# Interleaving the small products of a blocked triangular inverse over tiles of the PE array

## The chip, the cores and the metric

One core of one Trainium2 chip runs the kernel. The metric is the device time of one execution, in microseconds. The kernel before the change was run three times: 1209.91, 1213.57 and 1215.92 us, median 1213.57 us.

## What is computed

The reference is one block of a transformer: modulated norm, two token mixers, a gated output product and a feed-forward network, for 512 tokens of `x` with 1024 channels and 256 tokens of context. The part that matters here is the second mixer, the gated delta rule, which runs over chunks of the tokens in both directions. Each chunk needs the inverse of a unit lower triangular matrix (the reference solves with it in chunks of 64):

```python
m = jnp.where(strict, jnp.einsum('nbhid,nbhjd->nbhij', kb, k) * gamma, 0.0)
t_inv = lax.linalg.triangular_solve(eye + m, jnp.broadcast_to(eye, m.shape), left_side=True, lower=True)
w_c = t_inv @ (kb * jnp.exp(gc)[..., None])
u_c = t_inv @ (v * beta[..., None])
def update(s, w_i, u_i, kd_i, ge_i):
    v_new = u_i - jnp.einsum('bhck,bhkv->bhcv', w_i, s)
    s_next = s * jnp.exp(ge_i)[..., None, None] + jnp.einsum('bhck,bhcv->bhkv', kd_i, v_new)
    return v_new, s_next
```

The scan over the chunks is run once for the context, whose final states start the scan over `x`.

## The kernel before, in words

The kernel works with chunks of 128 tokens and float32 products (dense products as three products of split operands). The delta rule is done in six groups of heads: `c0` and `c1` (four heads of the context each) and `x0` to `x3` (two heads of `x` each). A group has eight chunk matrices forward and eight backward. For each group the program runs, in this order of the text:

- `k_prep`: norms of the keys and the triangular matrices `YF` (forward) and `YB` (backward).
- `substitution`: the inverses of all 32x32 diagonal blocks, for two groups at once, as 30 steps on the vector engine (two instructions each, names `x0t`/`x0pr`, `x2t`/`x2pr`), with transfers to DRAM and back before and after (`c2` holds the inverses, `cT` their transposes).
- `levels` (line 1011): the inverses grow from 32 to 64 to 128. First 32-wide: `pz` (32 products, a 32x32 block of `Y` times `cT`), copied to `zt`, then `px` (48 products of `zt` and `c2`), copied into `YF` (forward inverse), `XB` (backward inverse) and `XV` (the transposes that the next level needs). The inverted diagonal blocks themselves are copied into `YF`, `XB` and `XV` too (twelve small copies, lines 1054 to 1057). Then 64-wide: `pz2` (eight products a direction), copied into the free halves of `YB` (line 1065), then `px2` (eight a direction), copied into `YF` (line 1077) and `XB` (line 1079). The trace gives a tile's name without its last number, so `pz2` is listed with `pz`, and `px2` with `px`; the shape 32x32 or 64x64 tells them apart.
- `scan`: chunk by chunk, the products `ks`, `qs`, `xr` (with the inverse), `ds` and `ow`, with small evictions between them (`R`, `vb`, `w`, `S`, `o`).

In this stretch the tensor engine keeps the order of the program's text. The steps of the delta rule wait on each other, so pieces of the dense stream (the k, q, v, z and gate products `b`, 128x512 each) are laid between them: `cover(place)` lays as many microseconds of it as the table `COVER` says for the place (`c1l` is the place between the steps of `levels` of group `c1`). Inside `levels`, `turn()` calls it. `pump(us)` moves a clock of the program's text on; what hangs on that clock (steps of a substitution, weight splits, transfers) is written into the text when its time has come, so a smaller `pump` puts such work later in the text. Copies through `so` and `vo` keep their place on the scalar and vector engine as well; each engine works its queue in order.

A product that reads 32 partitions and writes 32 partitions uses one 32x32 tile of the array: the tile's row is set by the partitions that its operands lie on, its column by the partitions of the result. Before the change `pz` runs all sixteen products of one tile (operands on partitions 0 to 31, result on 32 to 63) and then all sixteen of another (64 to 95, 96 to 127); `pz2` has both directions on one tile of 64x64 (operands on the lower 64 partitions, results on the upper).

Of the kernel before, what the change touches and what calls it, by code (L numbers as in the profile page):

```python
# [17 lines left out]
P = 128  # L18
# [8 lines left out]
# columns of the packed per-channel vectors  # L27
# [12 lines left out]
# constant matrices  # L40
# [3 lines left out]
# how much of the dense products is laid at each place between the steps of the delta rule  # L44
# [15 lines left out]
    "c0l": (0, 4.13, 0, 4.59, 1.61, 2.63,),  # L60
# [6 lines left out]
    "c1l": (0, 0.99, 0, 2.0, 1.23, 0.99,),  # L67
# [9 lines left out]
    "x0l": (0, 1.57, 0, 2.37, 1.38, 0,),  # L77
# [12 lines left out]
    "x1l": (0, 3.58, 0, 2.81, 1.95, 0,),  # L90
# [7 lines left out]
    "x2l": (0, 0.65, 0, 2.31, 1.31, 0,),  # L98
# [6 lines left out]
    "x3l": (0, 1.12, 0, 2.45, 1.0, 0,),  # L105
# [7 lines left out]
def block_kernel(ctx: ExitStack, tc: tile.TileContext, x, ctxin, vecs, consts, wmodA, wmodB, wk, wv, wq,  # L113
# [70 lines left out]
    class Wide:  # L184
        """two pages side by side"""
# [49 lines left out]
    AB = sm([P, 8, 4], "AB")  # A_x, A_c, B_x, B_c per channel tile: A = g (1 + scale), B = shift  # L235

    class ModPart:
        """channel tiles c0 .. c0 + nt - 1, both conditions: the shift, and with rows the scale too, as rows on the
        tensor engine; else the scale as partial sums on each partition; added up as columns"""
# [26 lines left out]
        def columns(self):  # L266
            """columns of pt: the shift (tile, condition), then the scale: (tile, condition) or (condition, tile)"""
# [9 lines left out]
        def part(self, c):  # L277
            """A and B of condition c"""
# [71 lines left out]
    # mixer A's v goes two k-tiles at a time while the rest of the modulation comes in  # L350
# [13 lines left out]
    def av_part(b, w, i, js=None):  # L364
        """two of the first four k-tiles; w holds these two alone"""
# [123 lines left out]
    # spatial weights, transposed: wst[j, g, i]  # L489
# [72 lines left out]
    def gates(act, nt, name):  # L562
        n = nt * 8
# [14 lines left out]
        # g = -exp(a_log) * softplus(ba + dt_bias)  # L578
# [77 lines left out]
    def tab(*a, **k):  # L656
        """functions that change the scalar engine's table keep their order"""
# [10 lines left out]
    class Group:  # L668
        """some heads of x or of the context; a page holds 512 / n heads (four chunks of 128 tokens)"""
# [924 lines left out]
def _ch(v):  # L1594
    """[.., n*128] -> [128, .. * n]"""
    return v.reshape(-1, P).T
# [58 lines left out]
```

## Time and profile before

| what | before |
|---|---|
| median of 3 runs | 1213.57 us (1209.91 to 1215.92) |
| span of the profiled execution | 1209.3 us |
| median less span | 4.3 us |
| TensorE (PE) busy | 1174.6 us, 97% of the span |
| VectorE (DVE) busy | 711.6 us, 59% |
| ScalarE (ACT) busy | 599.8 us, 50% |
| GpSimd (POOL) busy | 222.6 us, 18% |
| PE's share of the chain that ended last | 87% |

The profiled execution's own device time is not listed apart from its span; what lies around a span can only be told from the runs, whose fastest is 0.6 us and whose median is 4.3 us above it. Busy times overlap, so an engine's share tells little by itself; the chain that ended last follows the work back from the last instruction, and its lines in order of time say which engine each stretch waited for.

### The profile page before, as it was taken

Reading aid. Unit: us, or ns where it says so; the run is one execution under the profiler, and the core shown is the slowest. Engines: PE = TensorE matmul, PEld = TensorE weight load, DVE = VectorE, ACT = ScalarE, POOL = GpSimd, SP = SyncE. Lnnn points to the kernel's source line nnn. Section 1 sums busy time; section 2 is a strip of 40 time slices with the busy share of each in tenths; the row PEclk is TensorE's granted clock in tenths of the full one; section 3 lists DMA queues with packets and bytes.
Section 4 is the critical chain, followed back from the end, with each engine's and each line's share of the span. In section 5 each row is a group of like instructions: output and inputs, shape, how many; then the busy total and the mean of one; then the engine's idle time right before and its main releaser. Section 6 shows DMA issues by size and latency. Waiting matters only on the chain.

```text
span 1209.3 us, 20707 instructions
## 1 busy us (share of the span) xinstructions
PE 1174.6 (97%) x7964; PEld 1017.8 (84%) x7964; DVE 711.6 (59%) x1481; ACT 599.8 (50%) x1299; POOL 222.6 (18%) x380
## 2 busy tenths in 40 slices
PE   6999999999799999999999999999999999999997
PEld 2798788789688888888888887899888888889997
DVE  2845784537487586565796558776645454543442
ACT  4345253647774745568656473356534343331332
POOL 1330000106650454226521211000000000000020
PEclk9999899999899999999999999999999999999999
DMA  8784843232354322113234222575432222223321
GB/s 295 237 285 152 283 145 138 105 109 101 106 165 137 99 81 79 54 53 96 80 105 141 63 96 70 195 256 189 146 105 90 103 99 93 104 88 96 114 88 70
DMA packets 76904, 154.52 MB, mean 128 GB/s; under 512 B 30083, under 2 KB 36099, under 8 KB 76806
## 3 DMA queue, kind: packets, MB, share of 16 engines
q1 hardware_dynamic: 75078, 150.06, 37.5%
q10 hardware_dynamic: 1728, 3.15, 0.7%
q8 instruction: 62, 1.02, 0.3%
q14 instruction: 36, 0.29, 0.1%
HBM read 138.50 MB, written 14.68 MB: 127 GB/s over the span
## 4 chain that ended last, share of the span: by engine, by line
PE 87%; DVE 3%; ACT 3%; DMA 3%; issue 2%; POOL 2%; SPq 1%; ACTq 0%; DVEq 0%; POOLq 0%
PE v L814 5%; PE dn L1535 3%; PE dn L1534 3%; PE dn L1533 3%; PE b L814 3%; PE z L814 3%; PE k L814 3%; PE q L814 3%; PE fa L209 3%; PE fb L209 3%; PE fb L211 3%; PE fa L211 3%; PE fa L210 3%; PE fb L210 3%; PE wo L229 1%
## 5 line engine op out<-in xcount | busy, mean ns | idle before, releaser
L181 ACT CAST whi<-wr 128x512 fp32r<-128x512 f32 x216 | 133.3, 621 | 285.0 <-PE fa L210 62.1
L182 DVE TENSOR_TENSOR wlo<-wr,whi 128x512 fp32r<-128x512 f32 x200 | 137.2, 690 | 187.5 <-ACT whi L181 186.8
L1567 POOL TENSOR_TENSOR fj<-x2r,fg 128x768 f32<-128x768 f32 x4 | 7.7, 1954 | 437.2 <-DVE x2r L1562 437.2
L1534 PE MATMUL dn<-wlo,gh 128*128 128x256 f32 x288 | 81.5, 283 | 0.0
L1535 PE MATMUL dn<-whi,gl 128*128 128x256 f32 x288 | 81.5, 283 | 0.0
L1533 PE MATMUL dn<-whi,gh 128*128 128x256 f32 x288 | 81.5, 283 | 0.0
L209 PE MATMUL fa<-h2h,whi 128*128 128x512 f32 x160 | 62.3, 389 | 0.0
L210 PE MATMUL fa<-h2l,whi 128*128 128x512 f32 x160 | 62.3, 389 | 0.0
L211 PE MATMUL fa<-h2h,wlo 128*128 128x512 f32 x160 | 62.2, 389 | 0.0
L209 PE MATMUL fb<-h2h,whi 128*128 128x512 f32 x160 | 62.2, 389 | 0.0
L210 PE MATMUL fb<-h2l,whi 128*128 128x512 f32 x160 | 62.2, 389 | 0.0
L211 PE MATMUL fb<-h2h,wlo 128*128 128x512 f32 x160 | 62.2, 389 | 0.0
L1533 PEld LDWEIGHTS dn<-whi,gh 128*128 128x128 f32 x288 | 55.3, 192 | 0.0
L1534 PEld LDWEIGHTS dn<-wlo,gh 128*128 128x128 f32 x288 | 55.3, 192 | 0.0
L1535 PEld LDWEIGHTS dn<-whi,gl 128*128 128x128 f32 x288 | 55.3, 192 | 0.0
L662 ACT ACT_TABLE_LOAD x39 | 50.0, 1283 | 7.4 <-DVE cvk L753 3.0
L429 DVE SCALAR_TENSOR_TENSOR mac<-wmb,cond,mac 128x1024 f32<-128x1024 f32 x30 | 39.3, 1312 | 4.5 <-DMA wmb<-wmodB 4.1
L229 PE MATMUL av<-whi,hxh 128*128 128x256 f32 x128 | 36.8, 288 | 0.7 <-ACT hxh L325 0.7
L231 PE MATMUL av<-whi,hxl 128*128 128x256 f32 x128 | 36.3, 285 | 1.1 <-DVE hxl L326 1.1
L230 PE MATMUL av<-wlo,hxh 128*128 128x256 f32 x128 | 36.2, 283 | 0.0
L211 PEld LDWEIGHTS fa<-h2h,wlo 128*128 128x128 f32 x160 | 30.1, 188 | 6.3
L211 PEld LDWEIGHTS fb<-h2h,wlo 128*128 128x128 f32 x160 | 30.0, 188 | 6.3
(1517 smaller groups left out, 3646.3 us busy)
## 6 DMA issues: line engine op xcount, KB each, us to landing
wr<-wup SPq DMA_DIRECT2D x42, 512.0 KB, 3.3
wmb<-wmodB SPq DMA_DIRECT2D x32, 512.0 KB, 6.7
wr<-wout SPq DMA_DIRECT2D x16, 512.0 KB, 3.9
wr<-wdn SPq DMA_DIRECT2D x16, 512.0 KB, 3.5
wm<-wmodA SPq DMA_DIRECT2D x16, 256.0 KB, 5.8
x<-x SPq DMA_DIRECT2D x8, 512.0 KB, 6.5
wm<-wmodA SPq DMA_DIRECT2D x8, 512.0 KB, 6.0
wr<-wu SPq DMA_DIRECT2D x8, 512.0 KB, 3.4
```

The costliest lines, as they stand in the source:

```text
L181: nc.scalar.copy(dst_hi, src)
L182: eng.tensor_tensor(dst_lo, src, dst_hi.bitcast(F32), op=ALU.subtract)
L209: mm(ps, lhsT=lh, rhs=rh, start=start, stop=False)
L210: mm(ps, lhsT=lh, rhs=rl, start=False, stop=False)
L211: mm(ps, lhsT=ll, rhs=rh, start=False, stop=stop)
L229: mm(ps, lhsT=a, rhs=wh[:, s], start=first and k == 0, stop=False)
L429: nc.vector.scalar_tensor_tensor(a, raw, cond[:, k, 0:1], a, op0=ALU.mult, op1=ALU.add)
L662: ins = nc.scalar.activation(*a, **k)
L814: tc.keep_in_program_order(mm(*a, **k))
L1533: mm(pss4[t][:, :256], lhsT=a, rhs=wh[:, s], start=k == 0, stop=False)
L1534: mm(pss4[t][:, :256], lhsT=a, rhs=wl[:, s], start=False, stop=False)
L1535: mm(pss4[t][:, :256], lhsT=c, rhs=wh[:, s], start=False, stop=k == NF - 1)
```

## The change

The same products are computed, and as many copies are made. In `levels` four things change.

- The loops are turned inside out. `pz` alternates between its two tiles, `px` between three, and `pz2` and `px2` between the two directions.
- The backward product of `pz2` is written to the lower 64 partitions; its copy into `YB` moves it to the upper 64.
- Copies start when all products of a stage are laid, no longer when half of them are. The second of the two `zt` copies goes from the scalar to the vector engine. The twelve copies of the diagonal blocks come behind `pz`; before they came behind `px`.
- `turn()` is called four times instead of six, and the table loses the two zeros, so the dense stream gets the same times at the same four places (after `pz`, `px`, `pz2`, `px2`). `pump` gets 0.6 four times, where it got 0.4 or 0.6 eight times.

Comments and docstrings are dropped elsewhere. The diff, cut to its core:

```diff
-    "c1l": (0, 0.99, 0, 2.0, 1.23, 0.99,),
+    "c1l": (0.99, 2.0, 1.23, 0.99),
...
-    "x0l": (0, 1.57, 0, 2.37, 1.38, 0,),
+    "x0l": (1.57, 2.37, 1.38, 0),
...
         pz = [chb(f"{name}pz{j}") for j in range(2)]
-        for j in range(2):
-            a, b = 2 * j, 2 * j + 1
-            sa, sb = slice(32 * a, 32 * a + 32), slice(32 * b, 32 * b + 32)
-            for m in range(16):
-                Y3 = YF3 if m < 8 else YB3
+        for m in range(16):
+            Y3 = YF3 if m < 8 else YB3
+            for j in range(2):
+                sa, sb = blk32[2 * j], blk32[2 * j + 1]
                 pmm(pz[j][sb, m * 32:m * 32 + 32], lhsT=Y3[sa, m % 8, sb], rhs=cT[sa, m], start=True, stop=True)
-            pump(0.4)
-            sc.copy(zt[sb].rearrange("p m c -> p (m c)"), pz[j][sb])
-            turn()
+        pump(0.6)
+        for j, copy in enumerate((sc.copy, ve.tensor_copy)):
+            sb = blk32[2 * j + 1]
+            copy(zt[sb].rearrange("p m c -> p (m c)"), pz[j][sb])
+        for bb in range(4):
+            bs = blk32[bb]
+            so.copy(YF3[bs, :, bs], c2[bs, Fm])
+            so.copy(XB3[bs, :, bs], cT[bs, Bm])
+            lb = slice(32 * (bb % 2), 32 * (bb % 2) + 32)
+            vo.tensor_copy(XV3[bs, :, lb], cT[bs, Fm] if bb < 2 else c2[bs, Bm])
+        turn()
         px = [scb(f"{name}px{j}") for j in range(2)]
-        for j in range(2):
-            a, b = 2 * j, 2 * j + 1
-            sa, sb = slice(32 * a, 32 * a + 32), slice(32 * b, 32 * b + 32)
-            for m in range(16):
-                ms = slice(m * 32, m * 32 + 32)
-                fwd = m < 8
+        for m in range(16):
+            ms = slice(m * 32, m * 32 + 32)
+            fwd = m < 8
+            for j in range(2):
+                sa, sb = blk32[2 * j], blk32[2 * j + 1]
                 if fwd or j == 1:
                     pmm(px[j][sa, ms], lhsT=zt[sb, m], rhs=c2[sb, m], start=True, stop=True)
                 if (not fwd) or j == 0:
                     pmm(px[j][sb, ms], lhsT=c2[sb, m], rhs=zt[sb, m], start=True, stop=True)
-            pump(0.6)
+        pump(0.6)
+        for j in range(2):
...
-            for bb in (a, b):
-                bs = slice(32 * bb, 32 * bb + 32)
-                so.copy(YF3[bs, :, bs], c2[bs, Fm])
-                so.copy(XB3[bs, :, bs], cT[bs, Bm])
-                lb = slice(32 * (bb % 2), 32 * (bb % 2) + 32)
-                vo.tensor_copy(XV3[bs, :, lb], cT[bs, Fm] if bb < 2 else c2[bs, Bm])
-            turn()
+        turn()
...
-        for d in range(2):
-            pz2 = scb(f"{name}pz2{d}")
-            for s in range(8):
-                pmm(pz2[hi64, s * 64:s * 64 + 64], lhsT=(YF3, YB3)[d][lo64, s, hi64], rhs=XV3[lo64, s] if d == 0 else XB3[lo64, s, lo64], start=True, stop=True)
-            pump(0.4)
-            (sc.copy if d == 0 else ve.tensor_copy)(z2[d][hi64], p3(pz2, 8)[hi64])
+        pz2 = [scb(f"{name}pz2{d}") for d in range(2)]
+        for s in range(8):
+            ss = slice(s * 64, s * 64 + 64)
+            pmm(pz2[0][hi64, ss], lhsT=YF3[lo64, s, hi64], rhs=XV3[lo64, s], start=True, stop=True)
+            pmm(pz2[1][lo64, ss], lhsT=YB3[lo64, s, hi64], rhs=XB3[lo64, s, lo64], start=True, stop=True)
+        pump(0.6)
+        sc.copy(z2[0][hi64], p3(pz2[0], 8)[hi64])
+        ve.tensor_copy(z2[1][hi64], p3(pz2[1], 8)[lo64])
         turn()
...
+        px2 = [scb(f"{name}px2{d}") for d in range(2)]
+        for s in range(8):
+            ss = slice(s * 64, s * 64 + 64)
+            pmm(px2[0][lo64, ss], lhsT=z2[0][hi64, s], rhs=YF3[hi64, s, hi64], start=True, stop=True)
+            pmm(px2[1][hi64, ss], lhsT=XV3[hi64, s], rhs=z2[1][hi64, s], start=True, stop=True)
+        pump(0.6)
```

How the rows of two engines move, in group `c1` and in group `x0`. On the tensor engine the products of `pz2` of group `c1` stand so before (`c1pz` is their result, `c1XV`, `c1XB`, `c1YF`, `c1YB` the operands; `z` is the dense stream, behind it `px2`):

```order
L814 MATMUL c1pz_4674<-c1XV,c1YF 64x64 x8
L814 MATMUL c1pz_4687<-c1XB,c1YB 64x64 x8
```

and so in the change, the first eight of sixteen:

```order
L814 MATMUL c1pz_4671<-c1XV,c1YF 64x64
L814 MATMUL c1pz_4672<-c1XB,c1YB 64x64
L814 MATMUL c1pz_4671<-c1XV,c1YF 64x64
L814 MATMUL c1pz_4672<-c1XB,c1YB 64x64
L814 MATMUL c1pz_4671<-c1XV,c1YF 64x64
L814 MATMUL c1pz_4672<-c1XB,c1YB 64x64
L814 MATMUL c1pz_4671<-c1XV,c1YF 64x64
L814 MATMUL c1pz_4672<-c1XB,c1YB 64x64
```

Forward and backward alternate now; `pz`, `px` and `px2` change in the same way, and the dense pieces between the four stages keep their number and place in every group. In `x3`, whose stages also have products `pb` of the next phase between them, 23 of these stand ahead of the scan before the change, and 25 in it.

On the vector engine, behind the last product of the scan of `c0` (`c02s1ds`, whose results update the states `c02s0S`), the queue at `levels(c1)` is before:

```order
L1170 SCALAR_TENSOR_TENSOR c02s0S_4435<-c02s0S_4435,cexs,c02s1ds 128x128
L1170 SCALAR_TENSOR_TENSOR c02s0S_4437<-c02s0S_4437,cexs,c02s1ds 128x128
L649 TENSOR_TENSOR x0t_4576<-x0pr 128x228
L1045 COPY c1YF<-c1px_4583 32x8x32
L991 TENSOR_TENSOR x0pr<-x0pr,x0t_4576 128x12x19
L1045 COPY c1YF<-c1px_4584 32x8x32
L649 TENSOR_TENSOR x0t_4609<-x0pr 128x220
L1048 COPY c1XV<-c1px_4583 32x8x32
L991 TENSOR_TENSOR x0pr<-x0pr,x0t_4609 128x11x20
L649 COPY c1XV<-c1cT 32x8x32 x2
```

and in the change:

```order
L1172 SCALAR_TENSOR_TENSOR c02s0S_4432<-c02s0S_4432,cexs,c02s1ds 128x128
L1172 SCALAR_TENSOR_TENSOR c02s0S_4434<-c02s0S_4434,cexs,c02s1ds 128x128
L1033 COPY c1zt<-c1pz_4535 32x512
L649 COPY c1XV<-c1cT 32x8x32 x2
L649 COPY c1XV<-c1c_4233 32x8x32 x2
L649 TENSOR_TENSOR x0t_4586<-x0pr 128x234
L991 TENSOR_TENSOR x0pr<-x0pr,x0t_4586 128x13x18
L1055 COPY c1YF<-c1px_4592 32x8x32
L649 TENSOR_TENSOR x0t_4642<-x0pr 128x228
L1055 COPY c1YF<-c1px_4593 32x8x32
L991 TENSOR_TENSOR x0pr<-x0pr,x0t_4642 128x12x19
L1058 COPY c1XV<-c1px_4592 32x8x32
```

A copy of `zt`, for which `px` waits, now stands behind the state updates, and the substitution of `x0` is one step later in the queue.

On the scalar engine, behind the last eviction of `v_prep(x0)` (`x0v`), the queue at `levels(x0)` is before:

```order
L662 ACT_TABLE_LOAD
L662 ACTIVATE b_5054<-b_4895 128x512
L649 CAST wq1hi<-wq1r 128x512
L1030 COPY x0zt<-x0pz_5075 32x512
L1030 COPY x0zt<-x0pz_5076 32x512
L1046 COPY x0XB<-x0px_5126 32x8x32
L649 COPY x0YF<-x0c_4907 32x8x32
L649 COPY x0XB<-x0cT 32x8x32
```

and in the change:

```order
L662 ACT_TABLE_LOAD
L662 ACTIVATE b_5054<-b_4895 128x512
L649 CAST wq1hi<-wq1r 128x512
L1033 COPY x0zt<-x0pz_5075 32x512
L649 COPY x0YF<-x0c_4935 32x8x32
L649 COPY x0XB<-x0cT 32x8x32
L649 COPY x0YF<-x0c_4935 32x8x32
L649 COPY x0XB<-x0cT 32x8x32
```

One `zt` copy is gone from this queue, the other still stands behind the table load, and the eight diagonal copies (four shown) come ahead of the copies out of `px`.

## Rows read from the trace of the kernel before

**Rows 1.** From the page: the tensor engine's busy time, share of the span and instructions, and the shares of the chain that ended last by engine.

```profile
PE 1174.6 (97%) x7964; PEld 1017.8 (84%) x7964; DVE 711.6 (59%) x1481; ACT 599.8 (50%) x1299; POOL 222.6 (18%) x380
...
PE 87%; DVE 3%; ACT 3%; DMA 3%; issue 2%; POOL 2%; SPq 1%; ACTq 0%; DVEq 0%; POOLq 0%
```

**Rows 2.** Busy time by stretch, for `levels` of `c1` and `x0`, and the sum over the six stretches of `levels`. Columns: stretch, its length, then busy us and instructions of PE, PEld (weight loads), DVE, ACT and POOL, PE's granted clock, DMA share, GB/s.

```profile
443.70:457.10 13.40, 13.40 (x247) 11.44 (x246) 10.27 (x26) 6.75 (x16) 4.47 (x7) 1.00 0.18 61
482.90:497.80 14.90, 14.90 (x253) 12.70 (x253) 7.23 (x14) 11.17 (x25) 4.16 (x10) 1.00 0.27 73
...
sum 96.10, PE 96.00 PEld 81.04 DVE 53.15 ACT 66.47 POOL 31.97; mean PE 16.00 PEld 13.51 DVE 8.86 ACT 11.08 POOL 5.33
```

**Rows 3.** The chain that ended last, in order of time, over `levels(c1)`. Columns: start us, us, what, and how many records (a float32 product is two records).

```profile
443.71 2.04 PE c1pz L814 x64
445.75 1.36 PE z L814 x5
447.11 2.04 PE c1px L814 x96
449.15 2.49 PE z L814 x10
451.64 2.02 PE c1pz L814 x32
453.66 1.58 PE z L814 x6
455.25 1.82 PE c1px L814 x32
```

**Rows 4.** Single records of the tensor engine in `px` (first two) and at the change of direction in `px2` (last two) of `c1`, in order of time. Columns: start us, us, engine, line, operation, result and operands, tile, shape.

```profile
447.12 0.19 PE L814 MATMUL c1px<-c1c,c1zt 32*32 32x32 f32 x1
447.13 0.19 PE L814 MATMUL c1px<-c1zt,c1c 32*32 32x32 f32 x1
...
455.93 0.27 PE L814 MATMUL c1px<-c1YB,c1XV 64*64 64x64 f32 x1
455.98 0.22 PE L814 MATMUL c1px<-c1YF,c1YB 64*64 64x64 f32 x1
```

**Rows 5.** The tensor engine alone by stretch: most of the first half of `pz` of `c1` (one tile), and the first 32 records of `px` of `c1` (eight forward matrices, two tiles in turn). Columns: stretch, length, busy us and records, granted clock, DMA share, GB/s.

```profile
443.64:444.62 0.98, 0.98 (x34) 1.00 0.39 134
447.04:447.54 0.50, 0.50 (x32) 1.00 0.90 369
```

**Rows 6.** Vector and scalar engine at `levels(c1)`, in order of time. Columns as in rows 4; in brackets the idle time before and what ended it.

```profile
444.88 0.59 DVE L649 TENSOR_TENSOR x0t<-x0pr 128x234 f32<-128x234 f32 x1
...
446.14 0.59 DVE L1170 SCALAR_TENSOR_TENSOR c02s0S<-c02s0S,cexs,c02s1ds 128x128 f32<-128x128 f32 x2
...
449.21 0.42 DVE L1045 COPY c1YF<-c1px 32x256 f32<-32x256 f32 x1 [0.21 <-PE c1px L814]
...
450.96 0.57 DVE L649 COPY c1XV<-c1cT 32x256 f32<-32x256 f32 x2
...
453.70 0.69 DVE L1065 COPY c1YB<-c1pz 64x512 f32<-64x512 f32 x1 [0.68 <-PE c1pz L814]
```

**Rows 7.** Scalar engine at `levels(x0)`, in order of time.

```profile
481.60 2.18 ACT L962 ACTIVATE x0v<-x0vt,xrk 128x128 f32<-128x128 f32 x8
483.80 1.28 ACT L662 ACT_TABLE_LOAD   x1
485.10 0.60 ACT L662 ACTIVATE b<-b 128x512 f32<-128x512 f32 x1
485.59 0.61 ACT L649 CAST wq1hi<-wq1r 128x512 fp32r<-128x512 f32 x1
486.23 1.18 ACT L1030 COPY x0zt<-x0pz 32x512 f32<-32x512 f32 x2
...
489.13 0.41 ACT L649 COPY x0YF<-x0c 32x256 f32<-32x256 f32 x1
...
489.85 0.41 ACT L649 COPY x0YF<-x0c 32x256 f32<-32x256 f32 x1
```

**Rows 8.** The chain that ended last over the end of `levels(x0)`: `px2`, and the first product with the inverse.

```profile
495.90 1.83 PE x0px L814 x32
...
499.94 0.11 PE x00s0xr L814
```

**Rows 9.** Vector engine at the end of `levels(x0)`, in order of time.

```profile
495.79 0.75 DVE L752 SCALAR_TENSOR_TENSOR cvq<-q,vec,cvq 128x511 f32<-128x511 f32 x1 [0.25 <-ACT cvq L749]
...
497.95 0.70 DVE L1079 COPY x0XB<-x0px 64x512 f32<-64x512 f32 x1
498.85 0.35 DVE L1134 SCALAR_TENSOR_TENSOR x00s0R<-x00s0ks,xexs,x0v 128x128 f32<-128x128 f32 x1 [0.20 <-PE x00s0ks L814]
```

**Rows 10.** Scalar engine at `levels(x3)`: the copy out of `pz2` and the squares behind it.

```profile
718.56 0.58 ACT L1065 COPY x3YB<-x3pz 64x512 f32<-64x512 f32 x1
719.17 1.15 ACT L1189 ACTIVATE osq<-o 128x512 f32<-128x512 f32 x2
```

**Rows 11.** The tensor engine's edge between the dense stream and `px` in `c1`: two dense products and the first small one.

```profile
446.48 0.40 PE L814 MATMUL z<-hxh,wz7lo 128*128 128x512 f32 x1
446.71 0.40 PE L814 MATMUL z<-hxh,wz7hi 128*128 128x512 f32 x1
447.04 0.21 PE L814 MATMUL c1px<-c1c,c1zt 32*32 32x32 f32 x1
```

More of the change, by code (lines that the diff above doesn't have):

```diff
@@ L59 @@
     "x1p": (0,),
-    "c0l": (0, 4.13, 0, 4.59, 1.61, 2.63,),
+    "c0l": (4.13, 4.59, 1.61, 2.63),
     "c00s2": (0.83, 0.8,),
@@ L89 @@
     "x3p": (0,),
-    "x1l": (0, 3.58, 0, 2.81, 1.95, 0,),
+    "x1l": (3.58, 2.81, 1.95, 0),
     "x12s1": (1.06, 0.67, 1.69, 1.72,),
@@ L97 @@
     "og": (0.29, 4.73, 0.08, 9.7, 1.3, 1.3, 1.3, 1.3,),
-    "x2l": (0, 0.65, 0, 2.31, 1.31, 0,),
+    "x2l": (0.65, 2.31, 1.31, 0),
     "x24s1": (0.18, 0.51, 0.42, 0.2,),
@@ L104 @@
     "x3v": (1.66, 0,),
-    "x3l": (0, 1.12, 0, 2.45, 1.0, 0,),
+    "x3l": (1.12, 2.45, 1.0, 0),
     "x36s1": (0, 0, 0, 0.13,),
@@ L1021, in levels @@
         zt = pg("gr", f"{name}zt").rearrange("p (m c) -> p m c", m=16)
+        blk32 = [slice(32 * i, 32 * i + 32) for i in range(4)]
         pz = [chb(f"{name}pz{j}") for j in range(2)]
-        for j in range(2):
-            a, b = 2 * j, 2 * j + 1
-            sa, sb = slice(32 * a, 32 * a + 32), slice(32 * b, 32 * b + 32)
-            for m in range(16):
-                Y3 = YF3 if m < 8 else YB3
-                pmm(pz[j][sb, m * 32:m * 32 + 32], lhsT=Y3[sa, m % 8, sb], rhs=cT[sa, m], start=True, stop=True)
-            pump(0.4)
-            sc.copy(zt[sb].rearrange("p m c -> p (m c)"), pz[j][sb])
-            turn()
-        px = [scb(f"{name}px{j}") for j in range(2)]
-        for j in range(2):
-            a, b = 2 * j, 2 * j + 1
-            sa, sb = slice(32 * a, 32 * a + 32), slice(32 * b, 32 * b + 32)
-            for m in range(16):
-                ms = slice(m * 32, m * 32 + 32)
-                fwd = m < 8
+        for m in range(16):
+            Y3 = YF3 if m < 8 else YB3
+            for j in range(2):
+                sa, sb = blk32[2 * j], blk32[2 * j + 1]
+                pmm(pz[j][sb, m * 32:m * 32 + 32], lhsT=Y3[sa, m % 8, sb], rhs=cT[sa, m], start=True, stop=True)
+        pump(0.6)
[9 more added lines that the diff above has]
+        turn()
+        px = [scb(f"{name}px{j}") for j in range(2)]
+        for m in range(16):
[3 more added lines that the diff above has]
+                sa, sb = blk32[2 * j], blk32[2 * j + 1]
                 if fwd or j == 1:
@@ L1066, in levels @@
-        turn()
-        for d in range(2):
-            px2 = scb(f"{name}px2{d}")
-            for s in range(8):
-                ss = slice(s * 64, s * 64 + 64)
-                if d == 0:
-                    pmm(px2[lo64, ss], lhsT=z2[d][hi64, s], rhs=YF3[hi64, s, hi64], start=True, stop=True)
-                else:
-                    pmm(px2[hi64, ss], lhsT=XV3[hi64, s], rhs=z2[d][hi64, s], start=True, stop=True)
-            pump(0.4)
-            if d == 0:
-                sc.copy(YF3[lo64, :, hi64], p3(px2, 8)[lo64])
-            else:
-                ve.tensor_copy(XB3[hi64, :, lo64], p3(px2, 8)[hi64])
+        pz2 = [scb(f"{name}pz2{d}") for d in range(2)]
@@ L1080, in levels @@
+        pump(0.6)
+        sc.copy(YF3[lo64, :, hi64], p3(px2[0], 8)[lo64])
+        ve.tensor_copy(XB3[hi64, :, lo64], p3(px2[1], 8)[hi64])
         turn()
@@ L1089, in block_kernel @@
     class Chain:
+        pass
     def feed(g, heads, step):
```

1 line of the change is left out of this document (added).

## The prediction

> **What bounds the kernel now.** I read the page first, then the busy time by stretch, the chain of waits, and single records. The page gives the tensor engine 97% of the span and 87% of the chain [rows 1]. In the six stretches of `levels` together it is busy 96.00 of 96.10 us, the vector engine 53.15 and the scalar engine 66.47 [rows 2]; nothing waits visibly. So in these stretches the tensor engine is the bound, and a shorter stream of products shortens the kernel, as long as the copies between the four stages stay hidden under the dense pieces.
>
> The stages themselves: in `c1` `pz` holds the engine 2.04 us, `px` 2.04, `pz2` 2.02 and `px2` 1.82, with 5, 10 and 6 dense products between them [rows 3]: 7.92 us a group, 47.5 us in six groups. These 224 records are short of work: in `pz`, all on one tile, 34 records take 0.98 us, some 30 ns each, while in the part of `px` that already takes two tiles in turn 32 take 0.50 us, 15.6 ns each [rows 5]. Single records show how: two on different tiles start 0.01 us apart, each 0.19 us long [rows 4].
>
> **The change, part by part.** *Products.* `pz`: 64 records on two tiles at 30 ns a tile and record are 32 x 0.031 = 1.0 us; with the edge 1.04, so 1.0 saved. `pz2`: 32 records on one tile are 2.0 us; on two tiles 1.02, so 1.0 saved. `px2`: its directions already lie on two tiles, and where one takes over from the other they overlap: the backward direction starts at 455.93, before a forward record at 455.98 [rows 4]. Alternating all the way gives some 0.95, so 0.87 saved. `px` mixes: today half of it alternates. With three tiles in turn its fullest tile has 32 records, so the floor is 1.0 us; if records never come closer than 15.6 ns its 96 take 1.5 us. I take 1.25, as starts 0.01 us apart leave room for a third tile: 0.79 saved. Sum 3.7 us a group, between 3.4 and 3.95.
>
> Here a rule speaks against the change. The 64-wide pairs read the same partitions and differ in the columns of the array, and so do the pairs in `px` that run at 15.6 ns [rows 5]. The Trainium skill ("TensorE: Matmul & The Clock Gate", part 3, The mechanism) says that a weight load overlaps with products in flight only when the row group differs. By that rule `pz2` and `px2` would stay at 2.0 and 1.8 us; the trace disagrees for the 32-wide pairs, and the overlap at 455.93 disagrees for the 64-wide.
>
> *Copies.* None is added. What changes is the start: copies wait for the whole stage, and the stage is shorter, so against the end of a stage nothing is lost. One `zt` copy moves from the scalar engine (0.59 us a copy [rows 7]) to the vector engine; nearest prices there are 0.42 us for half its columns and 0.69 for as many [rows 6]; I take 0.65. The copy that moves 64 partitions to the other half has no row; 0.69 is its floor, twice that its ceiling, and I take 0.69, since only the start partition differs. The ceiling would cost up to 0.7 us where it is waited for, 4.2 in all. The twelve diagonal copies leave the way from `px` to `pz2`, good, but the eight on the scalar engine (0.72 us a pair [rows 7]) now stand ahead of whatever comes next there.
>
> *Where the cover no longer reaches*, replayed in the clock of the old trace:
>
> `c0`, `x1`: their dense pieces are long (over 3 us after `pz` and `px`); the replay finds nothing exposed. 3.6 each.
>
> `c1`: `pz` would end at 444.75 and five dense products let `px` start at 446.1. But the new `zt` copy stands on the vector engine behind the state updates, the last of which end at 446.7 [rows 6]; so `zt` is there at 447.3, and `px` starts no sooner than now (447.11). That eats the whole saving of `pz`. Then `px` ends near 448.6, four `XV` copies (0.57 us for two [rows 6]), four substitution instructions and three evictions of some 0.4 us each bring `XV` to about 451.1; `pz2` starts at 451.2, 0.4 before today. Its backward copy, behind three more substitution instructions and a weight split, is done near 454.1; `px2` runs from 454.2 to 455.15 and today ends at 457.07. Saved: 1.9 of 3.7. Queued behind the waiting copy on that engine is the substitution of `x0`, one step later than before; its result is needed only at `x0pz`, some 30 us later.
>
> `x0`: `zt` on the scalar engine is behind the evictions of `v`, a table load, a sigmoid and a cast, which end at 486.23 and none of which wait for `pz` [rows 7]; so `px` starts at 486.9, where it is 487.07 now. `px` to 488.15, twelve dense products (2.96), `pz2` to 492.1, seven (1.81), `px2` to 494.9 instead of 497.73 [rows 8]. Then the vector engine binds: two taps, a split and the `XB` copy run back to back from 495.79 to 498.65 [rows 9]; the taps follow the dense block's end, about 1.7 us behind `pz2`, so the row moves to 493.8 and ends at 496.7, four `R` at 0.26 follow, and the first product with the inverse starts at 497.9 instead of 499.94. Saved: 2.0.
>
> `x2`: the diagonal copies (2.9 us) delay a weight cast and the split behind it, and with it `XV`, 0.3 us past the cover. Saved: 3.4.
>
> `x3`: the copy out of `pz2` waits behind eight diagonal copies (2.9), a table load (1.3), a sigmoid (0.6), two `XB` (0.7), squares (0.6 [rows 10]) and two casts (1.2), so it runs when it does today, at 718.6 [rows 10]; what of `pb` is pulled ahead counts as saved. 3.0.
>
> Sum: 3.6 + 1.9 + 2.0 + 3.6 + 3.4 + 3.0 = 17.5 us. The smaller `pump` only moves substitution steps one place later; everything else shifts along. The profiled span of 1209.3 would become 1191.8; the median of the runs stands 4.3 above that span, and 1213.57 - 17.5 = **1196.0 us**.
>
> **Rivals.** (A) The forecast.
>
> (B) Everything stays hidden: my replays are too strict, for instance because the vector engine starts a copy earlier than I put it. 6 x 3.7 = 22 us, 1191.4. For it: no wait shows today [rows 2]. Against: the two queues in the order of the change.
>
> (C) The copies bind in most groups, as in `c1` and `x0` or worse (the shifted 64-partition copy at its ceiling, more queueing on the scalar engine): 1.0 to 1.9 us a group, 6 to 11 us, about 1205. For it: the scalar engine is busy 11.17 of 14.90 us in `x0` [rows 2], and after the change of 11.2.
>
> (D) Only pairs on different partitions overlap (the rule above). As a mechanism here: `pz` saves 1.0, the third tile in `px` 0.5, the 64-wide stages nothing, and in `c1` and `x0` `pz`'s part is lost: about 6 us, 1207. Against: rows 4 and 5.
>
> (E) The change does not do what it says: the engine takes its queue strictly in order and the alternation is not used. Then the products cost what they cost, and the lost head start of the first half's copies adds about 1 us: 1214.6. Against: rows 4.
>
> (F) Slower. Each change of tile costs what the edge between dense and small products costs: 0.33 us from start to start instead of 0.23 [rows 11], 0.1 us. `pz` would have some 32 changes, `px` 48, `pz2` and `px2` 16 each: 112 x 0.1 = 11.2 us a group against 7.9, 20 us more in all, 1233. It decides once the mean spacing over the 224 records passes 35 ns. Against: `px` changes its tile at nearly every record at 15.6 ns.
>
> **How the numbers follow.** A 0.58, B 0.12, C 0.18, D 0.04, E 0.04, F 0.04. A, B and most of C (0.15) lie more than 0.5% (6.1 us) below today, which is about what a measurement of this kernel can tell from no change: faster 0.85. The rest of C with D and E: same 0.11. Slower 0.04. The range reaches from all hidden with `px` at its floor (6 x 3.95 = 23.7 us, 1190) to the weaker part of C, 7.5 us saved: 1190 to 1206.
>
> **What would show it.** In the changed profile `pz` should take about 1.0 us for 64 records, `px` 1.0 to 1.5 for 96, `pz2` 1.0 and `px2` 0.95 for 32. `px` of `c1` should wait for the vector engine's `zt`, `px` of `x0` for the scalar engine's, `xr` of `x0` for `R`. The stretch from the first `pz` to the scan should shrink by 3.5 us in `c0` and `x1` and by about 2 in `c1` and `x0`, and what lies between the groups should keep its length. The prediction is wrong if the 64-wide stages keep 2 us (D), if records alternate at 30 ns (E), or if waits of some us appear ahead of `px` or `px2` in all groups (C).

## The result, and the profile after

The changed kernel takes 1194.57 us (median of 4 runs, 1192.69 to 1199.92) against 1211.97 before: a ratio of 0.9875, 95% interval 0.9848 to 0.9902. A second comparison, of 6 runs with 11, gave 0.9896 (0.9875 to 0.9917). The prediction was 1196.0, within 1190 to 1206. The change makes the kernel faster: by 15.1 us in the first comparison and 12.6 in the second. The forecast of 17.5 was too high, by 3.6 us against the 13.9 that the traces show below, and its median came nearer than its sum deserved.

The page's two lines that answer to [rows 1]:

```profile
PE 1152.9 (97%) x7964; PEld 995.5 (84%) x7964; DVE 714.5 (60%) x1487; ACT 595.8 (50%) x1293; POOL 223.2 (19%) x380
...
PE 83%; DVE 5%; ACT 4%; DMA 4%; issue 2%; POOL 2%; SPq 1%; ACTq 0%; POOLq 0%; DVEq 0%
```

The tensor engine is busy 21.7 us less (some 4 of them belong to the first trace of the kernel before alone, in which the clock fell once more; its second trace has 1170.8); its share of the chain falls from 87 to 83%, and the vector engine's rises from 3 to 5%. The products became cheap enough for copies to be waited for. The stages, in the chain of the changed kernel over `levels(x1)`, where the tensor engine waits for nothing (columns as in rows 3):

```profile
565.26 1.13 PE x1pz L814 x64
...
570.47 1.14 PE x1px L814 x95
...
575.00 1.08 PE x1pz L814 x32
...
578.58 1.08 PE x1px L814 x32
```

4.43 us, where [rows 3] add up to 7.92. The single records of the first two products of `pz2` show why (start us, us):

```profile
574.93 0.27 PE L814 MATMUL x1pz<-x1XV,x1YF 64*64 64x64 f32 x1
574.94 0.27 PE L814 MATMUL x1pz<-x1XB,x1YB 64*64 64x64 f32 x1
575.04 0.22 PE L814 MATMUL x1pz<-x1XV,x1YF 64*64 64x64 f32 x1
575.05 0.22 PE L814 MATMUL x1pz<-x1XB,x1YB 64*64 64x64 f32 x1
```

Forward and backward start 0.01 us apart. But the tensor engine now waits in the stretches, where it waited for nothing [rows 2]. Its waits there, and one in the scan of `x1` (us in total, times, longest):

```profile
PE c1pz L814 <- DVE c1XV L1058: 1.1, 1, 1.1
...
PE x0pz L814 <- ACT x0v L962: 0.8, 1, 0.8
PE c1px L814 <- DVE c1zt L1033: 0.7, 1, 0.7
...
PE x12s1ks L814 <- DVE c02s0S L1172: 0.6, 1, 0.6
...
PE x2pz L814 <- DVE x2XV L1058: 0.4, 1, 0.4
PE x3pz L814 <- DVE x3XV L1058: 0.3, 1, 0.3
```

**A ruler that is finer than the runs.** Runs scatter by several us; the starts of single products do not, once counted from the first product of `pz` in `c0`. The table gives us from the first product of a group's `pz` to its first product with the inverse (`xr`), from the first `xr` of `x1` to `pz` of `x2`, and the stretch from the first `pz` of `c0` to the first product of the feed-forward. Everything that the change touches lies in that stretch. The other columns belong to the experiments below.

| | before | after | loops_only | one_half | grain | wide | mixed_now |
|---|---|---|---|---|---|---|---|
| c0 | 23.0 | 19.5 | 20.2 | 20.5 | 20.8 | 19.3 | 19.6 |
| c1 | 14.7 | 13.5 | 11.6 | 14.1 | 13.6 | 13.6 | 11.6 |
| x0 | 17.0 | 14.4 | 15.3 | 15.3 | 15.7 | 15.4 | 13.4 |
| x1 | 21.1 | 17.4 | 18.4 | 18.3 | 18.8 | 18.6 | 17.4 |
| x1 `xr` to x2 `pz` | 54.5 | 56.0 | 54.5 | 54.8 | 55.9 | 54.5 | 56.3 |
| x2 | 15.7 | 12.9 | 13.0 | 13.7 | 13.6 | 12.6 | 12.8 |
| x3 | 17.8 | 15.7 | 14.5 | 16.5 | 15.8 | 13.9 | 13.5 |
| stretch | 458.4 | 444.5 | 444.1 | 449.5 | 448.1 | 442.9 | 440.3 |

By this ruler the change saves 13.9 us: 15.9 in the six groups, less 1.5 in the scan of `x1` and some 0.5 elsewhere. The other 3.9 us between the two profiled spans lie ahead of `pz` of `c0`. The ruler has a limit: a fall of the granted clock inside the stretch lengthens it. The two traces each of the kernel before and of the change show none there; some of the experiments below do, and it is said beside them.

### The profile page after: what moved, and what is told of

Its sections match the earlier page's. It is cut to its first block, busy times and chain, and to the rows that moved or that the text cites. A ratio compares the mean times of both kernels' runs of the same rounds, so it can differ in the third digit from the quotient of the medians.

```text
span 1191.7 us, 20707 instructions
## 1 busy us (share of the span) xinstructions
PE 1152.9 (97%) x7964; PEld 995.5 (84%) x7964; DVE 714.5 (60%) x1487; ACT 595.8 (50%) x1293; POOL 223.2 (19%) x380
## 3 DMA queue, kind: packets, MB, share of 16 engines
q8 instruction: 62, 1.02, 0.4%
## 4 chain that ended last, share of the span: by engine, by line
PE 83%; DVE 5%; ACT 4%; DMA 4%; issue 2%; POOL 2%; SPq 1%; ACTq 0%; POOLq 0%; DVEq 0%
PE v L814 5%; PE dn L1537 4%; PE dn L1536 4%; PE dn L1535 4%; PE k L814 3%; PE z L814 3%; PE b L814 3%; PE fa L209 3%; PE fa L210 3%; PE fb L209 3%; PE fb L210 3%; PE fb L211 3%; PE fa L211 3%; PE q L814 3%; PE ga L209 1%
## 5 line engine op out<-in xcount | busy, mean ns | idle before, releaser
L209 PEld LDWEIGHTS fb<-h2h,whi 128*128 128x128 f32 x160 | 30.1, 188 | 6.3
```

The lines of the kernel that those rows point to most:

```text
L209: mm(ps, lhsT=lh, rhs=rh, start=start, stop=False)
```

## The experiments

**How much of the difference is the change's.** Both kernels once more, unedited.

> The changed kernel once more, to size its gain better. In the two traces at hand the stretch from the first product of pz in c0 to the first product of the feed-forward took 458.4 us before and 444.5 us with the change, 13.9 less, while another 3.9 us of the difference lie ahead of that first product, where both kernels do the same. Theory T (what lies ahead is the scatter of single executions: the granted clock was 0.69 at 139 to 150 us in the execution before and 1.00 in the one after): the stretch is again 444.5 within 0.5, and the median of the differences between runs is nearer 14 than 17.4 us, a ratio of 0.988. Rival N (the change does speed up what lies ahead, by the placement of its tiles, for instance): the first product of pz in c0 again stands at 395.9, and the ratio is 0.9855, 17.5 us.

> The kernel before once more, for its trace. Theory T: no drop of the granted clock at 139 to 150 us, so the first product of pz in c0 stands near 396.5 instead of 399.8, and the stretch from there to the feed-forward is 458.4 us within 0.5. Rival N: 399.8 again.

Measured: stretch 444.2 for the changed kernel and 458.3 for the one before, each within 0.3 us of its first trace. The first `pz` of `c0` came at 395.5 and 396.5. T holds: the 399.8 of the first trace belongs to that execution. In the runs below that product comes between 394.7 and 401.6, though no edit touches what lies ahead of it, so 1 us there is scatter. Busy time by stretch of the kernel before, in its first trace (first two rows) and in the second (the last two):

```profile
139.00:145.00 6.00, 6.00 (x25) 5.08 (x24) 4.92 (x7) 0.62 (x1) 0.00 (x0) 0.57 0.95 304
145.00:150.00 5.00, 5.00 (x27) 4.24 (x26) 2.33 (x4) 1.15 (x2) 0.00 (x0) 0.83 0.62 254
```

```profile
139.00:145.00 6.00, 6.00 (x36) 4.95 (x37) 5.60 (x9) 0.62 (x1) 0.00 (x0) 1.00 0.94 297
145.00:150.00 5.00, 5.00 (x31) 4.29 (x30) 4.01 (x9) 1.58 (x3) 0.00 (x0) 1.00 0.74 297
```

The granted clock of the first 6 us was 0.57 in one execution and 1.00 in the other (the two levels are 0.50, 1.2 GHz, and 1.00, 2.4 GHz); 52 records against 67 in the same 11 us. The run grain below has the fall too (0.63 in these 6 us), and the same 399.8.

**The loops without the copies' new places.** The copies go back to where they were, and `pump` gets its old sums:

```diff
-        for j, copy in enumerate((sc.copy, ve.tensor_copy)):
+        for j in range(2):
...
-            copy(zt[sb].rearrange("p m c -> p (m c)"), pz[j][sb])
-        for bb in range(4):
...
+            sc.copy(zt[sb].rearrange("p m c -> p (m c)"), pz[j][sb])
...
+            for bb in (2 * j, 2 * j + 1):
...
```

> The four loops alternate and the backward pz2 lands in the other half, but the copies stay where they were (both zt copies on the scalar engine, the diagonal copies behind px) and pump gets its old sums (0.8, 1.2, 0.8, 0.8). Theory T (the products save 3.5 us a group; what c1 gave away of that, 2.3 us, is the zt copy behind the state updates on the vector engine, what x2 gave away, 0.7, the diagonal copies on the scalar engine, and the 1.4 us that x1's scan lost come from the substitution of x2 standing later on the vector engine): px of c1 no longer waits, c1 saves 2.5 to 3.5 instead of 1.2, x2 3.4 instead of 2.8; in x0 px waits for the second zt copy, saving 2.0. In x1's scan a step of the substitution now stands between the R instructions, and if its data has not landed by then, xr is late by up to 4 us. Stretch from pz of c0 to the feed-forward: 442 to 446 us. Rival C (the products themselves wait for copies wherever these stand, since they all have to be done before pz2): c1 and x2 save no more than with the change, the stretch is 445 to 448.

Measured: stretch 444.1, ratio to before 0.9884 (0.9866 to 0.9902), the same as the change. But the groups differ. `c1` saves 3.1 instead of 1.2, `x3` 3.3 instead of 2.1, and `x1`'s scan loses nothing. `c0`, `x0` and `x1` lose 0.7 to 1.0 each, and `x2` is no better (2.7). T holds for `c1` and for the scan, and is wrong on `x2`. The copies' move is worth nothing in sum: it helps three groups and harms two, and the six groups together take 93.0 us here and 93.4 in the change. The scan of `x1` is 1.5 better here, but 1.0 more lies between `c0` and `c1` (21.8 for 20.8). Where the move helps, these waits of the tensor engine stand in loops_only, gone in the change:

```profile
PE c00s0xr L814 <- DVE c0XB L1081: 0.6, 1, 0.6
PE x1pz L814 <- ACT x1XB L649: 0.6, 1, 0.6
PE c0px L814 <- ACT c0YB L1071: 0.5, 1, 0.5
```

With the diagonal copies behind `px`, `pz2` of `x1` waits for one of them (`x1XB`, L649).

**The smaller `pump`.** `pump(0.6)` four times becomes 0.8, 1.2, 0.8, 0.8; nothing else.

> The changed kernel, but pump gets the old sums (0.8, 1.2, 0.8, 0.8 instead of 0.6 four times), so the steps of the substitutions stand about one earlier on the vector engine. Theory T: the 1.4 us that x1's scan lost behind the first product with the inverse come down to 0.3 or less, since the weight split moves out from between the state updates; the wait for XV in c1 grows by 0.3, as one more step of x0's substitution stands ahead. Stretch from pz of c0 to the feed-forward 443.4 us, 1.1 less than 444.5. Rival (the smaller pump is without weight, x1's scan is late because the transfer for x2's substitution lands late in real time): x1's scan still loses 1.0 or more, stretch 444.5.

Measured: stretch 445.9, ratio 0.9873 (0.9859 to 0.9888). The span from the first `xr` of `x1` to `pz` of `x2` stayed at 56.4, so T falls: it is not the `pump`. (Of the 1.4 us by which the stretch is longer than the change's, 0.9 lie behind the first `xr` of `x3`, where the granted clock was 0.51 from 731.2 to 734.7.) The first step of `x2`'s substitution started at 586.8, where it starts in the change. The vector engine there, in the changed kernel:

```profile
585.78 0.35 DVE L1172 SCALAR_TENSOR_TENSOR c02s0S<-c02s0S,xexs,x12s0ds 128x128 f32<-128x128 f32 x1 [3.77 <-PE x12s0ds L814]
586.69 0.17 DVE L649 TENSOR_TENSOR x2t<-x2pr 128x30 f32<-128x30 f32 x1 [0.56 <-issue]
...
586.78 0.34 DVE L1172 SCALAR_TENSOR_TENSOR c02s0S<-c02s0S,xexs,x12s0ds 128x128 f32<-128x128 f32 x1
...
587.14 0.68 DVE L649 TENSOR_TENSOR wb3lo<-wb3r,wb3hi 128x512 fp32r<-128x512 f32 x1
...
587.87 0.34 DVE L1172 SCALAR_TENSOR_TENSOR c02s0S<-c02s0S,xexs,x12s0ds 128x128 f32<-128x128 f32 x1
...
588.26 0.34 DVE L1172 SCALAR_TENSOR_TENSOR c02s0S<-c02s0S,xexs,x12s0ds 128x128 f32<-128x128 f32 x1
```

and in the kernel before, four updates in a row:

```profile
600.42 1.12 DVE L1170 SCALAR_TENSOR_TENSOR c02s0S<-c02s0S,xexs,x12s0ds 128x128 f32<-128x128 f32 x4
```

From the start of the first, the updates now take 2.8 us instead of 1.1: a step of the substitution that waits 0.56 us, its second half, a weight split and another step came between them, and the next chunk's `ks` needs all four.

These are two causes, a wait and an order, and the traces can part them. The wait is for the transfer that brings the substitution's data. In rows_apart, a run below, the transfer was issued at 580.96 and took 4.4 us to land (last column), and the step starts 0.06 us behind that:

```profile
x2pr<-x2sc SPq DMA_DIRECT2D x1, 512.0 KB, 4.4
```

```profile
585.42 0.17 DVE L649 TENSOR_TENSOR x2t<-x2pr 128x30 f32<-128x30 f32 x1 [1.75 <-issue]
```

In the change the trace records the last part of the same transfer at 586.63 and in its second trace at 585.92, and the step starts 0.06 to 0.07 us later, as there. The order alone shows in grain, also below, where the transfer had landed at 591.61 and the step waits for nothing:

```profile
593.58 0.35 DVE L1177 SCALAR_TENSOR_TENSOR c02s0S<-c02s0S,xexs,x12s0ds 128x128 f32<-128x128 f32 x1 [3.88 <-PE x12s0ds L814]
593.88 0.23 DVE L649 TENSOR_TENSOR x2t<-x2pr 128x30 f32<-128x30 f32 x1
...
595.53 0.33 DVE L1177 SCALAR_TENSOR_TENSOR c02s0S<-c02s0S,xexs,x12s0ds 128x128 f32<-128x128 f32 x1
```

The four updates still take 2.3 us, and `x1`'s scan loses 1.4, 0.4 of which is waited at `pz` of `x2` for the substitution's end. So about 1.0 of the change's 1.5 us is the order, and the rest the wait. Of the rival, the half on the `pump` holds; the late transfer is the smaller part. What puts the steps between the updates stays open: one_half and rows_apart have the change's `pump` and copies, and their first step stands ahead of all four.

**The substitution later.** One edit, in `substitution`:

```diff
-        later(DMA1, lambda: step(30))
+        later(DMA1 + (4.0 if name == "x2" else 0), lambda: step(30))
```

> The changed kernel, but the substitution of x2 starts 4 us of the program's clock later, so its first step stands behind the four state updates of x1's first scan step on the vector engine instead of among them. Theory L (since levels of x1 is 3.7 us shorter and the transfer for the substitution takes its time regardless, the vector engine reaches the step before the data, and three state updates and the next products wait behind it): the time from the first product with the inverse in x1's scan to pz of x2 goes from 56.0 back to 54.5 us, the stretch from pz of c0 to the feed-forward from 444.4 to 443.0. Rival M (the substitution's end was about to bind: pz of x2 waits 0.3 for its data in one trace): what the scan gains is waited for at pz of x2, stretch 444.5 or more.

Measured: stretch 451.4, ratio 0.9942 (0.9921 to 0.9963). The rival M holds, and harder than put: the tensor engine waits for the end of the substitution.

```profile
PE x2pz L814 <- DVE x2cT L649: 6.1, 1, 6.1
```

Without that wait, the way from `xr` of `x1` to `pz` of `x2` would be 60.1 - 6.1 = 54.0 us, so what stood between the updates was indeed what held the scan (this edit takes the order and the wait away together). But the substitution was just in time: in the change's second trace `pz` of `x2` already waits 0.3 us for it. The wait is not all that the delay costs. Behind it the granted clock was 0.50, the lower level of 1.2 GHz:

```profile
641.60:651.80 10.20, 8.46 (x171) 6.94 (x172) 5.25 (x11) 4.75 (x12) 0.64 (x1) 0.50 0.31 101
```

The group `x2`, which lies there, took 15.9 us instead of 12.9: 3.0 of the 7.0 us by which the stretch is longer than the change's.

**One tile against two.** The backward `pz2` goes back to the upper partitions:

```diff
-            pmm(pz2[1][lo64, ss], ...
+            pmm(pz2[1][hi64, ss], ...
...
-        ve.tensor_copy(z2[1][hi64], p3(pz2[1], 8)[lo64])
+        ve.tensor_copy(z2[1][hi64], p3(pz2[1], 8)[hi64])
```

> The changed kernel, but the backward pz2 lands in the upper partitions again, on the tile of the forward one; the directions still alternate, in two PSUM banks, and the copy no longer moves partitions. Theory T (a tile works through its own products at 31 ns a record of 32 wide and 62 of 64 wide, different tiles work at the same time): pz2 takes 2.0 us again instead of 1.08, in all six groups, and the stretch from pz of c0 to the feed-forward grows by 0.9 x 6 = 5 us, to 449.5; the copy out of pz2 on the vector engine takes 0.70 as with the move. Rival E2 (what helps is that neighbours in the queue have different destinations, not different tiles): pz2 stays near 1.08 and the stretch at 444.4.

The chain over `pz2` of `c0` in this kernel:

```profile
407.03 2.00 PE c0pz L814 x32
```

Stretch 449.5, both as T said; the six groups together grew by 5.0. (The scan of `x1` lost 1.2 less than in the change, and what lies between and behind the groups took as much more; in the scan of `x3` the granted clock was 0.51 from 733.7 to 737.1.) Alternating alone does nothing on one tile, though the two directions write different banks: the other half of the partitions is what counts.

**Same rows or same columns.**

```diff
-            pmm(pz2[1][lo64, ss], lhsT=YB3[lo64, s, hi64], rhs=XB3[lo64, s, lo64], ...
+            pmm(pz2[1][hi64, ss], lhsT=YB3[hi64, s, hi64], rhs=XB3[hi64, s, hi64], ...
```

> The changed kernel, but the backward pz2 multiplies the blocks that lie on the upper partitions and writes to the upper partitions, so its values are not the inverse's. The pair now differs in the rows of the array and shares its columns and result partitions; in the changed kernel it shares the rows and differs in the columns. Theory T (any two tiles run side by side): pz2 1.08 us. Rival K (two tiles in the same columns share the way to the result, so they take turns): 2.0 us.

The chain at the same place:

```profile
408.54 1.08 PE c0pz L814 x32
```

K falls. Two tiles of 64x64 run side by side, whether they share rows (the change) or columns (here).

**How far ahead the engine looks.** The order of the products alone: `pz` and `pz2` in runs of two products a tile, `px` and `px2` in runs of four.

```diff
-        for s in range(8):
+        for d, s in [(d, s0 + i) for s0 in range(0, 8, 4) for d in range(2) for i in range(4)]:   # px2
```

> The changed kernel, with the products alternating in runs instead of one by one: pz and pz2 in runs of two products (four records) a tile, px and px2 in runs of four (eight records). Theory Q (each tile has its own waiting products, far ahead): all four stages keep their 1.1 us. Theory S (the queue is taken in order, a product waits at its head until its tile is free, so only the last of a run overlaps with the first of the next): pz 16 runs of 3 x 31 + 10 ns = 1.65 us, px 12 runs of 7 x 31 + 10 = 2.7, pz2 8 runs of 3 x 62 + 5 = 1.5, px2 4 runs of 7 x 62 + 5 = 1.75. That in the kernel before the two directions of px2 overlapped by only 0.05 us speaks for S.

The chain over `levels(c0)`:

```profile
399.83 1.15 PE c0pz L814 x64
...
405.74 2.05 PE c0px L814 x96
...
413.00 1.13 PE c0pz L814 x32
...
416.17 1.47 PE c0px L814 x32
```

Neither theory holds. Runs of two products cost next to nothing (1.15 and 1.13), as Q had it; in runs of four, `px` takes 0.9 us more than in the change and `px2` 0.4, each some six tenths of the loss that S expected. That is as if the engine looked past a run of two products and only part of the way into a run of four; the kernel before had runs of eight to sixteen on one tile. How it looks ahead no run shows.

**More tiles.** `pz` on four tiles in one bank, `px` on six:

```diff
-                pmm(pz[j][sb, m * 32:m * 32 + 32], lhsT=Y3[sa, m % 8, sb], rhs=cT[sa, m], start=True, stop=True)
+                    pmm(pz[sa if d else sb, i * 32:i * 32 + 32], lhsT=Y3[sa, m, sb], rhs=cT[sa, i], start=True, stop=True)
...
+                if j == 0:
+                    pmm(px[0][blk32[2], f], lhsT=c2[sb, m], rhs=zt[sb, m], start=True, stop=True)
+                else:
+                    pmm(px[1][blk32[0], b], lhsT=zt[sb, m + 8], rhs=c2[sb, m + 8], start=True, stop=True)
```

> The changed kernel with more tiles: pz on four instead of two (forward result where it was, backward result one block lower, all in one PSUM bank; the copies into zt become four of half the size, the backward ones move the partitions) and px on six instead of three (the products for XV land in a free block, their copies move the partitions). The fullest tile of either stage has 16 records instead of 32. Theory T: pz 64 records in 0.5 us and px 96 in 0.5, with the edges 0.6 each instead of 1.13; the single bank takes away x0's wait for the second one (0.8). Saved in full in c0 and x1 (2.1), 1.3 in x0, little in c1, x2 and x3, where copies bind: stretch from pz of c0 to the feed-forward 444.4 - 4 = 440.5 us. Rival I (the engine issues no more than one record each 10 ns): pz 0.75, px 1.1, stretch 442.5. Rival P (four tiles into one bank take turns): pz 2 us, stretch 447.

Stretch 442.9, ratio 0.9869 (0.9853 to 0.9886). The tensor engine alone, in `pz` of `x1` (first row) and in `px` of `c0` (columns as in rows 5):

```profile
572.05:572.45 0.40, 0.40 (x53) 1.00 0.00 0
407.55:408.25 0.70, 0.70 (x86) 1.00 0.00 0
```

Four tiles run at 0.40 / 53 = 7.5 ns a record, four times one tile's rate, so P falls. Six run at 0.70 / 86 = 8.1 instead of the 5.2 that T expects; I's 10 is too slow and T's sum too fast. None of it reached the groups, which together take 93.4 as in the change: the four copies into `zt` are longer, and `px` of `x0` waits 1.0 for the scalar engine's and 0.5 for the vector engine's. (In `c1` the granted clock was 0.50 from 446.9 to 450.3, so its 13.6 is too long by an unknown part.) The 1.6 that the stretch gained is the scan of `x1`, which loses nothing here: its updates stand together.

**Copies placed by group.** As the groups in loops_only and the change asked for, with the later substitution still in it; then with `pz` in one bank as well:

```diff
+        late = name in ("c1", "x3")
...
+            (ve.tensor_copy if name == "x0" or j and not late else sc.copy)(zt[sb]...
...
+        if not late:
+            diag(range(4))
...
+            if late:
+                diag((2 * j, 2 * j + 1))
```

> The version that the runs so far point to: the changed kernel with the copies placed by group. In c1 and x3 as before the change (both zt copies on the scalar engine, diagonal copies behind px), in x0 both zt copies on the vector engine, in the other groups as changed; and the substitution of x2 starts 4 us later as in the run beside it. Theory T, adding the better of the measured stretches group by group (first product of pz to first with the inverse): c0 19.5, c1 11.6 instead of 13.5, x0 13.9 instead of 14.4, x1 17.4, x2 12.9, x3 14.5 instead of 15.7, and 1.4 in x1's scan: 444.4 - 5.0 = 439.5 us for the stretch from pz of c0 to the feed-forward, median 5 us under the changed kernel's, near 1190. Rival W (groups pass on what they gain as waits, as dense products and weight splits of one group's time fall into the next): half of that, 442.

> As the run beside it, with both tiles of pz in one PSUM bank instead of two, so that in x0 the second tile's first product no longer waits 0.8 us for a bank that the evictions of v still hold. Theory T: pz of x0 takes 1.13 instead of 1.9 us and, since zt now is copied on the idle vector engine, x0 saves up to 0.5 more: stretch 439.0. Rival P (two tiles in one bank take turns): pz 2.0 us in every group, stretch 443 or more.

Both came to a stretch of 450.8, since both hold the delay, whose cost was not known yet (6.1 and 6.6 us waited at `pz` of `x2`, and 17.0 and 16.2 for `x2` behind it). By groups, `c1` came to 11.6 and 12.3, `x0` to 14.4 and 13.4, `x3` to 14.5 and 13.5. P falls: `pz` of `c0` takes 1.13 us with one bank too, and only with it does `x0` gain; why `c1` took 0.7 more stays open. So the last run takes the delay out and keeps one bank in `x0` and `x3`:

```diff
+        pz = [chb(f"{name}pz0")] * 2 if name in ("x0", "x3") else [chb(f"{name}pz{j}") for j in range(2)]
```

> The version with the copies placed by group (c1 and x3 as before the change, x0 with both zt copies on the vector engine, the others as changed), without the later substitution that cost 6 us at pz of x2, and with both tiles of pz in one PSUM bank in x0 and x3 alone. Theory T, from the stretches measured group by group, first product of pz to first with the inverse: c0 19.5, c1 11.6, x0 13.4, x1 17.4, x2 12.9, x3 13.5, where the changed kernel has 19.5, 13.5, 14.4, 17.4, 12.9 and 15.7, that is 5.1 less; given back 0.6 between c1 and x0 (25.0 instead of 24.4) and up to 1.6 behind x3 (135.1 instead of 133.5). Stretch from pz of c0 to the feed-forward 444.4 - 3.5 = 441 us, median some 3 us under the changed kernel's. Rival W (with the dense stream at the bound, what one group gains the next place waits for): 443.5 to 444.5, no difference that the runs can show.

Stretch 440.3, as T said, median 1193.33 against 1208.92 before in the same runs, ratio 0.9875 (0.9847 to 0.9903). In the trace it is 4.0 us shorter than the change (two traces, 444.5 and 444.2) and 18 shorter than before; the medians of the runs cannot tell it from the change.

## Why the prediction was right, and where its sum was not

| step | forecast | measured |
|---|---|---|
| `pz`, `px`, `pz2`, `px2` of a group | 1.04, 1.25, 1.02, 0.95 | 1.13, 1.14, 1.08, 1.08 |
| saved in products, a group | 3.66 | 3.49 |
| c0, x1 | 3.6, 3.6 | 3.5, 3.7 |
| c1 | 1.9 | 1.2 |
| x0 | 2.0 | 2.6 |
| x2 | 3.4 | 2.8 |
| x3 | 3.0 | 2.1 |
| between the groups | 0 | -2.0 |
| sum | 17.5 | 13.9 |

**Products: right.** Tiles run side by side at their own 31 or 62 ns a record, also for the 64-wide pair, for which there was only the overlap at 455.93 [rows 4]. The doubt over the third tile in `px` is settled: 1.14 is the fullest tile's 32 records with the edges, not 96 records at 15.6 ns. The rule weighed ahead (the Trainium skill, "TensorE: Matmul & The Clock Gate", part 3, The mechanism) would have kept `pz2` at 2.0 us as long as both directions read the same partitions; the trace disagrees, with 1.08. By the Trainium skill ("TensorEngine Tiling (Array Packing)", Key Properties), tiles operate independently; the runs agree up to four tiles, at 7.5 ns a record.

**The shifted copy: no extra price.** It took 0.68 us, where the copy that stays on its partitions took 0.69: the floor of the forecast.

**`c1`: right in kind, mis-sized by 0.7.** The vector engine there, for [rows 6]:

```profile
438.26 0.59 DVE L1172 SCALAR_TENSOR_TENSOR c02s0S<-c02s0S,cexs,c02s1ds 128x128 f32<-128x128 f32 x2
438.89 0.70 DVE L1033 COPY c1zt<-c1pz 32x512 f32<-32x512 f32 x1
439.62 0.83 DVE L649 COPY c1XV<-c1cT 32x256 f32<-32x256 f32 x2
440.46 0.59 DVE L649 COPY c1XV<-c1c 32x256 f32<-32x256 f32 x2
441.08 0.79 DVE L649 TENSOR_TENSOR x0t<-x0pr 128x234 f32<-128x234 f32 x1
...
443.97 0.42 DVE L1058 COPY c1XV<-c1px 32x256 f32<-32x256 f32 x1
```

The `zt` copy stands behind the state updates as forecast, and ends 0.3 us sooner than the replay put it, counted from the first `pz`. `px` starts ahead of it, stops after four records for 0.7 us and goes on. The vector engine then does not pause up to 444.4, and `pz2` starts 0.3 us later than before the change where 0.4 earlier was forecast: one step of the substitution alone took 0.79 instead of the 0.59 of [rows 6].

**`x0`: right at its start, wrong at its end.** The scalar engine's `zt` copy, for [rows 7]:

```profile
475.10 1.28 ACT L662 ACT_TABLE_LOAD   x1
...
476.89 0.61 ACT L649 CAST wq1hi<-wq1r 128x512 fp32r<-128x512 f32 x1
477.52 0.58 ACT L1033 COPY x0zt<-x0pz 32x512 f32<-32x512 f32 x1
```

It ends at 478.10, and `px` starts at 478.29, as long after the first `pz` as before: no head start, as forecast. The vector engine was expected to bind at the end; no wait stands there, so 0.6 more was saved. What the replay did not see is that `pz` now needs its second bank at once. That bank still held `v`: 0.8 us, hidden here because `zt` was late anyway. In mixed_now, where neither binds, `x0` takes 1.0 less.

**`x2`, `x3`: half seen.** `XV` of `x2` was 0.4 us past the cover, 0.3 forecast. In `x3`, `px2` does not run as one block. The tensor engine's records in the changed kernel:

```profile
702.74 0.32 PE L814 MATMUL x3px<-x3YF,x3YB 64*64 64x64 f32 x2
702.99 0.50 PE L211 MATMUL pb<-oz,wlo 128*128 128x512 f32 x1
...
703.65 0.27 PE L814 MATMUL x3px<-x3YB,x3XV 64*64 64x64 f32 x1
703.66 0.27 PE L814 MATMUL x3px<-x3YF,x3YB 64*64 64x64 f32 x1
```

One forward product starts it, two products of `pb` follow, and only then do the directions alternate. The backward copy out of `pz2` ends at 703.08, behind a sum of squares and a weight split on the vector engine. The forecast looked at the scalar engine alone.

**"Everything else shifts along": the step that failed.** The forecast has nothing between the groups; measured are 2.0 us, 1.5 of them in the scan of `x1`. There steps of `x2`'s substitution and a weight split came between the four state updates, about 1.0 us as grain shows without any wait, and the first step waited 0.56 for its data. The prediction counted by how many places the smaller `pump` moves such steps in the text, not what they then stand between, nor when their data would be there. The data came late on two counts. `levels(x1)` in front of the scan became 3.7 us shorter, and the transfer took 6.0 us from issue to landing where it took 3.2 before. It is now issued 0.4 us behind a block of weights of 512 KB, where it was issued 4.5 ahead of that block; that the block is the reason is argued, not shown.

**The median.** 1194.57 against 1196.0 looks better than 13.9 against 17.5, because the forecast was set against a trace with a clock drop of some 3 us ahead of the change and runs of that kind; in the later runs the kernel before took 1208.92 to 1210.47. That part of the hit is luck. The 4.3 us between span and median are scatter too: the profiled run of the change took 1193.42 us at a span of 1191.7, 1.7 more.

## What to carry to other kernels

Small products on one tile leave the rest of the array idle; alternate tiles product by product or in twos, and choose the result's partitions for that, since the copy out moved them at no cost here (0.68 us). Size such a change by the fullest tile's records, then replay each copy's queue, and then ask of every transfer and bank behind it whether it still arrives in time when its cover is shorter, and of every queue what now stands between two steps of a chain. To size a change of one per cent, count from a product that both traces share, not from the ends of the runs.

## What the runs showed of the hardware

Runs of two products a tile overlap like single ones, runs of four about half. Rates were 31 ns a record on one tile, 15.6 on two [rows 5], about 10.4 on three (two rounds of three in 0.06 us), 7.5 on four (`pz`) and 8.1 on six (`px`): beyond four tiles nothing was gained. The granted clock fell at 139 to 150 us in one execution of the kernel before and not in another, though the engine had waited 1.7 us just ahead of it in the first and 2.1 us in the second. Behind a wait of 6.1 us in delay it was 0.50 for 10 us. A step of the vector engine that waited for a transfer started 0.06 to 0.07 us behind its recorded landing (change, rows_apart).
